# A two-layer hybrid decoder trunk on one core: the last steps of the attention gates at the scheduler's highest priority

## The chip, the cores and the metric

The kernel runs on one core of one Trainium2 chip. The metric is the device time of one execution in microseconds (us), as the median of several runs; lower is better. The core's engines are named as in the profile: PE (TensorE matmul), PEld (its weight loads), DVE (VectorE), ACT (ScalarE), POOL (GpSimd) and SP (SyncE, which here issues nearly all DMAs). A "q" behind an engine's name stands for its sequencer, so SPq is the queue from which SP issues its DMAs, one behind the other.

## The reference, cut to what matters

Two layers, sequence 1024, width 1024, all in float32:

```
h    = rms_norm(x, pre_gain) * (1 + scale) + shift
proj = h @ w_in            # split into q, k, v and gate of three head groups
a_out = sliding_window_attention(aq, ak, av, sinks) * silu(ag)
r_out = rms_norm(retention(rq, rk, rv)) * silu(rg)
g_out = rms_norm(gated_linear_attention(...)) * silu(gg)
y    = concatenate([a_out, r_out, g_out]) @ w_out
x    = x + gate * rms_norm(y, post_gain)
```

The change touches only `* silu(ag)`: the product of the attention's output with its gate, 512 of the 1024 columns of the concatenation.

## The kernel before, in words

**Numbers.** Every matmul operand is held as a high part (`fp32r`, a rounded copy) and a low part (the value minus its high part), and a product is three passes: high by high, low by high, high by low. So each activation that goes into a matmul passes through a cast and a subtraction, both on DVE for the gates.

**Tiles.** The sequence is 8 token tiles of 128. The mixed activations of a tile go through DRAM: `mixS` holds them split in high and low part, `mixF` holds them whole (only in the last layer, for tiles 2 to 7), `aoS` holds the attention's output before its gate, `xs` the residual between the layers.

**Order.** The PE instructions stand in the order in which the program writes them. A small planner inside the program decides that order: each unit of work is a generator ("job") that yields a delay or a flag to wait for, and `pump()` runs the jobs that are due on a clock that counts PE time only. The instructions of the other engines, the DMAs of SP's queue included, are placed by the tile scheduler: it takes of the instructions that it thinks ready the one with the highest priority, by default the one written earliest. Within an engine's queue the order is then fixed, and each instruction waits there for its semaphores while those behind it wait too.

**The gates.** `gate(g, hf, kk, pm)` handles 128 of the 512 gate columns (`k = 2*g + kk`) for four token tiles (half `hf`). It takes the projection from PSUM (`tanh` on ACT, L1583, and a DVE step, L1584), waits until the attention's output of the four tiles is in `aoS`, loads it into `ao` (a DMA of 256 KB, `lao`), and after a further delay does its last steps:

- the product `ao = th * 0.5 * ao` (L1590, DVE);
- in the last layer the store of the whole values to `mixF` (tiles 2 to 7 only);
- the cast to the high part `mh` (`copy("mg")`, L151, DVE) and the low part `ml` (L1602, DVE);
- two stores, of `mh` and of `ml`, to `mixS`;
- the flags `mix1`, on which the planner lets the output product of these tiles begin.

There are 16 gates, eight in each layer. All their stores go through SP's queue (`sm0`, `sm1`).

**The last layer's end.** `last_output` multiplies tiles 0 and 1 plainly and tiles 2 to 7 in three pairs (`Pair`), each by seven block products on sums and differences of the blocks. A pair's `parts()` loads four whole blocks from `mixF` (256 KB each); `sum()` builds four sums on DVE (L1305 to L1308); `early()` and `late()` split them into high and low part (cast on ACT, L149; low part on DVE, L1279); `a22()` loads a block of `mixS` in two halves (`a<-mixS`). `kept` (L1341) copies a product out of PSUM on ACT, `summed` adds banks on DVE (L1345), takes the squares on ACT (L1349) and multiplies by the gain (L1350). `finish` loads the residual (`t<-xs`), adds on DVE (L1248) and stores the output on ACT's queue (`out_dram<-t`).

The tiles of the prediction: `t_2055` and `t_2056` are the last two gates' `ao` (tiles 4 to 7); `t_2058`, `t_2059`, `t_2060` and `t_2061` are the four blocks of the first pair (tiles 2 and 3); `t_2066` and `t_2067` are the residual of tile 0; `t_2002` and `t_2003` are the two gates before the last two.

Of the kernel before, what the change touches and what calls it, by code (L numbers as in the profile page):

```python
# [93 lines left out]
def trunk(ctx: ExitStack, tc: tile.TileContext, ins, cst, out):  # L94
# [18 lines left out]
    def t2(dt=F32):  # L113
        return gp.tile([P, 512], dt, tag="t2", name=nm("t2"), bufs=B2)
# [16 lines left out]
    def f(ap):  # L131
        return ap.bitcast(F32)
# [11 lines left out]
    def eng(k):  # L144
        return G if EN[k] == "G" else V

    def copy(k, dst, src):
        if EN[k] == "A":
            A.activation(dst, src, AF.Copy)  # L149
        else:  # L150
            V.tensor_copy(dst, src)  # L151

    def dma(k, dst, src):
        {"S": nc.sync, "A": A, "P": G}[EN[k]].dma_start(dst, src)
# [28 lines left out]
    def lat(key, l):  # L183

        return L[key + "@1"] if l and key + "@1" in L else L[key]
# [4 lines left out]
    def flag(name, lat=0.0):  # L190
        flags[name] = clk[0] + lat
# [1274 lines left out]
    def layer(l):  # L1466
# [35 lines left out]
        for p in range(NP_):  # L1502
            last = p == NP_ - 1
            rr = {}
            for name in ("rq", "rk", "rv"):
                w = used(l, name)
                for tt in range(2):
                    t = 2 * p + tt
# [68 lines left out]
        def rows(d, hf, *i):  # L1577
            return d[(slice(4 * hf, 4 * hf + 4), slice(None)) + i].rearrange("t p q -> p t q")

        def gate(g, hf, kk, pm):  # L1580
            k = 2 * g + kk
            th = t2()
            A.activation(th, pm, AF.Tanh, scale=0.5)  # L1583
            V.scalar_tensor_tensor(th, th, 1.0, pm, ALU.add, ALU.mult)  # L1584
            for t in range(4 * hf, 4 * hf + 4):
                yield (0.0, ("ao", l, t, g))
            ao = t2()
            dma("lao", ao.rearrange("p (t q) -> p t q", t=4), rows(aoS, hf, k))
            yield lat("ag1", l)
            V.scalar_tensor_tensor(ao, th, 0.5, ao, ALU.mult, ALU.mult)  # L1590
            mh, ml = t2(F32R), t2(F32R)
            def tiles(x, ts):
                return x.rearrange("p (t q) -> p t q", t=4)[:, ts]

            ts = slice(0, 4)
            if l == DEPTH - 1:
                t0 = max(PLAIN - 4 * hf, 0)
                if t0 < 4:
                    dma("sm0", rows(mixF, hf, k)[:, t0:4], tiles(ao, slice(t0, 4)))
                ts = slice(0, min(t0 + 1, 4)) if t0 else slice(0, 4, 2)  # L1600
            copy("mg", tiles(mh, ts), tiles(ao, ts))
            eng("mgl").tensor_tensor(tiles(ml, ts), tiles(ao, ts), tiles(f(mh), ts), ALU.subtract)  # L1602
            for a, m in ((0, mh), (1, ml)):
                dma(f"sm{a}", rows(mixS, hf, a, k)[:, ts], tiles(f(m), ts))
            for t in range(4 * hf, 4 * hf + 4):
                flag(("mix1", l, t, k), lat("lay1", l))

        for hf in range(2):
            for g in range(2):
# [7 lines left out]
        for hf in range(2):  # L1617
            for g in range(2):
                for kk in range(2):
                    pm = mm()  # L1620
                    project_T(pm, l, hf, used(l, f"ag{g}"), kk * P)
                    job(gate(g, hf, kk, pm))
                    pump()
                if hf and not g:
                    if l == DEPTH - 1:
                        sw_first("W10")
                    else:
                        load(l, "o2")
            if not hf:
                if l == DEPTH - 1:  # L1630
                    sw_first("T1")
                    sw_first("W11")
                else:
                    load(l, "o0")
                    load(l, "o1")
# [86 lines left out]
```

## Time and profile before

| what | value |
|---|---|
| time, median of 3 runs | 998.21 us (996.72 to 999.19) |
| the profiled execution's own time | 996.31 us |
| its span, first to last instruction | 994.6 us |
| mean granted TensorE clock | 0.991 |
| PE busy | 965.7 us, 97% of the span |
| DVE, ACT, POOL busy | 683.2, 409.3, 246.3 us |

Times inside the kernel are us from the span's start. The groups by line show what an instruction costs, the windows show how busy each engine is in a stretch, the chain shows the work that ended last, followed back from the last instruction. On the chain an entry gives its start and how long it lasted.

### The profile page before, as it was taken

To read this page: it belongs to the slowest core of one execution; us is meant where nothing else is said; L and a number is where in the kernel's file an instruction comes from. 1 tells how busy PE (TensorE), PEld (TensorE's weight loads), DVE (VectorE), ACT (ScalarE), POOL (GpSimd) and SP (SyncE) were. 2 spreads that over 40 slices of the span, in tenths; PEclk is the share of its full clock that TensorE was granted. 3 is DMA by queue.
4 is the path that set the end of the run, shared out by engine and by line. 5 is a ranking of instruction groups with operands and counts; after the bars stand their busy time and mean duration, and the time that the engine had idled before them with its cause. 6 is when DMAs were issued, how large, how long until landed. Compare 5 with 4: busy or idle time off the path is not lost.

```text
span 994.6 us, 19641 instructions
## 1 busy us (share of the span) xinstructions
PE 965.7 (97%) x7133; PEld 824.3 (83%) x7133; DVE 683.2 (69%) x1679; ACT 409.3 (41%) x1152; POOL 246.3 (25%) x310
## 2 busy tenths in 40 slices
PE   5899999999999999999999999999999999999996
PEld 1599999888998777778889999988999877777785
DVE  3779857677766777664677286775766577567876
ACT  2477312233332656632555332133333257574222
POOL 2322001233310234420124101113322034545000
PEclk8899999999999999999999999999999999999999
DMA  9843513523135355587555241352122434378883
GB/s 321 290 138 97 159 44 115 177 86 121 61 100 166 91 157 168 170 274 239 189 170 171 69 150 38 118 157 83 53 93 86 127 91 133 112 235 266 267 262 139
DMA packets 112305, 148.77 MB, mean 150 GB/s; under 512 B 12065, under 2 KB 63821, under 8 KB 112209
## 3 DMA queue, kind: packets, MB, share of 16 engines
q1 hardware_dynamic: 106512, 137.96, 44.5%
q10 hardware_dynamic: 5696, 9.56, 2.6%
q8 instruction: 56, 0.92, 0.4%
q14 instruction: 41, 0.33, 0.1%
HBM read 109.20 MB, written 36.18 MB: 146 GB/s over the span
## 4 chain that ended last, share of the span: by engine, by line
PE 80%; DVE 7%; DMA 7%; issue 2%; POOL 1%; ACT 1%; SPq 0%; ACTq 0%; POOLq 0%; DVEq 0%
PE mm L165 61%; PE aux L165 14%; PE aux L180 5%; DMA st<-in_w_in_dram 2%; POOL sm L635 1%; DMA t<-aoS 1%; DMA st<-in_w_last_dram 1%; DMA xk<-in_x_dram 1%; DVE arena L533 1%; DMA a<-mixS 1%; DVE t L1248 0%; DVE t L328 0%; DMA t<-in_x_dram 0%; DMA t<-xs 0%; DMA mixS<-t 0%
## 5 line engine op out<-in xcount | busy, mean ns | idle before, releaser
L165 PE MATMUL mm<-arena 128*128 128x256 f32 (+2 forms) x1824 | 299.9, 318 | 1.8 <-ACT arena L704 1.8
L165 PE MATMUL mm<-arena,arena 128*128 128x256 f32 (+2 forms) x1824 | 298.2, 316 | 0.0
L165 PEld LDWEIGHTS mm<-arena 128*128 128x128 f32 x1824 | 255.5, 191 | 26.0 <-issue 3.3
L165 PEld LDWEIGHTS mm<-arena,arena 128*128 128x128 f32 x1824 | 252.2, 188 | 24.3 <-issue 3.7
L635 POOL TENSOR_TENSOR sm<-sm,mhalf 128x1 f32<-128x1 f32 (+1 forms) x64 | 55.8, 872 | 335.9 <-DVE sm L634 317.8
L165 PE MATMUL mm<-arena,mx 128*128 128x512 f32 (+1 forms) x564 | 130.6, 387 | 0.5 <-ACT kept L1341 0.5
L165 PEld LDWEIGHTS mm<-arena,mx 128*128 128x128 f32 x564 | 101.4, 188 | 24.7 <-issue 1.9
L149 ACT ACTIVATE t<-aux 128x256 f32<-128x256 f32 (+2 forms) x124 | 55.8, 468 | 73.8 <-PE aux L180 62.2
L149 ACT ACTIVATE arena<-st 128x512 fp32r<-128x512 f32 x94 | 56.2, 627 | 53.2 <-DMA st<-in_w_in_dram 19.4
L929 POOL TENSOR_TENSOR smx<-smx,sm 128x512 f32<-128x512 f32 x32 | 36.1, 1129 | 125.7 <-DVE sm L928 118.0
L533 POOL TENSOR_TENSOR arena<-st,arena 128x512 fp32r<-128x512 f32 x31 | 42.7, 1378 | 79.7 <-ACT arena L149 72.9
L533 DVE TENSOR_TENSOR arena<-st,arena 128x512 fp32r<-128x512 f32 x77 | 58.0, 775 | 5.2 <-ACT arena L149 3.3
L925 ACT ACTIVATE smx<-smx,sm 128x129 f32<-128x129 f32 x128 | 49.9, 393 | 25.9 <-DVE sm L922 25.7
L364 DVE SCALAR_TENSOR_TENSOR acc<-st,c_act,acc 128x512 f32<-128x512 f32 x60 | 46.7, 778 | 16.9 <-DMA st<-in_w_mod_dram 16.5
L180 PE MATMUL aux<-c_ident,t 128*128 128x128 f32 (+1 forms) x292 | 48.2, 282 | 5.4 <-DVE t L666 5.0
L180 PEld LDWEIGHTS aux<-c_ident,t 128*128 128x128 f32 (+1 forms) x292 | 35.0, 144 | 12.4 <-DVE t L666 6.9
L698 ACT ACTIVATE t<-aux,mod,mod 128x128 f32<-128x128 f32 x68 | 25.9, 459 | 43.0 <-DVE t L1248 18.1
L165 PEld LDWEIGHTS aux<-t,mx 32*128 32x128 f32 (+1 forms) x896 | 39.5, 187 | 3.9 <-issue 2.1
L973 ACT ACTIVATE t<-aux 128x256 f32<-128x256 f32 x32 | 12.3, 383 | 73.6 <-PE aux L165 65.0
L165 PE MATMUL aux<-t,mx 32*128 32x32 f32 (+1 forms) x896 | 40.7, 272 | 0.0
L920 DVE COPY_PREDICATED smx<-c_curmask,aux 128x256 f32<-128x256 int32 x64 | 25.4, 446 | 19.5 <-ACT smx L149 17.2
L1248 DVE SCALAR_TENSOR_TENSOR t<-t,sm,t 128x512 f32<-128x512 f32 x32 | 24.0, 780 | 18.2 <-DMA t<-in_x_dram 10.8
(224 smaller groups left out, 1387.7 us busy)
## 6 DMA issues: line engine op xcount, KB each, us to landing
st<-in_w_in_dram SPq DMA_DIRECT2D x96, 256.0 KB, 3.8
st<-in_w_mod_dram SPq DMA_DIRECT2D x64, 256.0 KB, 3.1
mx<-mixS SPq DMA_DIRECT2D x20, 512.0 KB, 4.9
mixS<-t SPq DMA_DIRECT2D x72, 128.0 KB, 3.7
st<-in_w_last_dram SPq DMA_DIRECT2D x36, 256.0 KB, 3.8
wm<-in_w_mod_dram SPq DMA_DIRECT2D x12, 512.0 KB, 7.0
t<-in_x_dram SPq DMA_DIRECT2D x24, 256.0 KB, 4.9
t<-tabS SPq DMA_DIRECT2D x16, 256.0 KB, 4.6
```

What stands on the lines that cost most here:

```text
L149: A.activation(dst, src, AF.Copy)
L165: T.matmul(dst, lhsT, rhs, start=start, stop=stop)
L180: T.transpose(dst, src, idn)
L364: V.scalar_tensor_tensor(acc, wt, c_act[:, k:k + 1], acc, ALU.mult, ALU.add)
L533: e.tensor_tensor(lo, st, f(hi), ALU.subtract)
L635: G.tensor_tensor(r, r, mhalf[:, :w], ALU.pow)
L698: A.activation(hf[:, ks], at[kt], AF.Identity, scale=gain, bias=shift)
L920: V.copy_predicated(sv, curmask.unsqueeze(1).to_broadcast((P, 2, P)), pv[:, :, n // P - 1, :])
L925: A.activation(sm[:, h, :], sm[:, h, :], AF.Exp, bias=mx[:, h:h + 1], accum_out=sums[:, h:h + 1])
L929: eng("pn").tensor_tensor(sm[:, :, 0:128], sm[:, :, 0:128], rs.unsqueeze(2).to_broadcast((P, 4, P)), ALU.mult)
L973: A.activation(sq, po, AF.Square)
L1248: V.scalar_tensor_tensor(xt[j], yg[j], r, xt[j], ALU.mult, ALU.add)
```

## The change

The last steps become a function `gate_out`, and it is called inside `tc.high_priority()`: whenever the scheduler thinks one of these instructions ready, it places it ahead of every other ready instruction of that engine. Nothing else is edited: the same instructions with the same operands, and the PE order is the same word for word. (The low part's line becomes L1608, the product's L1596.)

```
             ao = t2()
             dma("lao", ao.rearrange("p (t q) -> p t q", t=4), rows(aoS, hf, k))
             yield lat("ag1", l)
+            with tc.high_priority():
+                gate_out(hf, k, th, ao)
+            for t in range(4 * hf, 4 * hf + 4):
+                flag(("mix1", l, t, k), lat("lay1", l))
+
+        def gate_out(hf, k, th, ao):
             V.scalar_tensor_tensor(ao, th, 0.5, ao, ALU.mult, ALU.mult)
             mh, ml = t2(F32R), t2(F32R)
...
             eng("mgl").tensor_tensor(tiles(ml, ts), tiles(ao, ts), tiles(f(mh), ts), ALU.subtract)
             for a, m in ((0, mh), (1, ml)):
                 dma(f"sm{a}", rows(mixS, hf, a, k)[:, ts], tiles(f(m), ts))
-            for t in range(4 * hf, 4 * hf + 4):
-                flag(("mix1", l, t, k), lat("lay1", l))
```

What moves is little: no row on PE and POOL, and a few rows at each gate on DVE and SP. Three places matter below.

SP's queue in the last layer, at the last two gates (`t_2055`, `t_2056`) and the first pair's loads (`t_2058` and up; `-` stands before, `+` now):

```order
 L154 DMA t_2056_11464<-aoS 128x4x128
 L154 DMA t_2058_11470<-mixF 128x512
+L154 DMA mixF<-t_2055_11462 128x4x128
+L154 DMA mixF<-t_2056_11464 128x4x128
 L154 DMA t_2059_11472<-mixF 128x512
 L154 DMA t_2060_11474<-mixF 128x512
@@ -579,6 +581,4 @@
 L154 DMA t_2066_11493<-xs 128x512
 L154 DMA t_2067_11494<-xs 128x512
-L154 DMA mixF<-t_2055_11462 128x4x128
-L154 DMA mixF<-t_2056_11464 128x4x128
```

The two stores moved ahead of the last three of the pair's four loads and of the two residual loads; on DVE no row moved around this place.

SP's queue one step earlier, at the two gates before these (`t_2002`, `t_2003`; `t_2012` to `t_2015` are their high and low parts; `st` are the last layer's weights on their way in):

```order
 L154 DMA mixF<-t_2003_11197 128x4x128
+L154 DMA mixS<-t_2012_11255 128x2x128
+L154 DMA mixS<-t_2014_11263 128x2x128
+L154 DMA mixS<-t_2013_11256 128x2x128
+L154 DMA mixS<-t_2015_11264 128x2x128
 L154 DMA aoS<-t_2011_11239 128x256
-L154 DMA mixS<-t_2012_11255 128x2x128
-L154 DMA mixS<-t_2013_11256 128x2x128
-L154 DMA mixS<-t_2014_11263 128x2x128
-L154 DMA mixS<-t_2015_11264 128x2x128
 L154 DMA st_11370<-in_w_last_dram 128x512
```

The four stores moved ahead of one store of the attention's output, and the weight load stands behind all five as before.

ACT's queue at the first pair (`mx_11501` and `mx_11581` are the high parts of the sums, `kept_11613` the copy of the pair's first product):

```order
 L149 ACTIVATE mx_11501<-t_2060_11474 128x512
+L149 ACTIVATE mx_11581<-t_2058_11470 128x512
 L154 DMA out_dram<-t_2066_11493 128x512
 L149 ACTIVATE mx_11581<-t_2061_11476 128x512
 L154 DMA out_dram<-t_2067_11494 128x512
-L149 ACTIVATE mx_11581<-t_2058_11470 128x512
+L1341 ACTIVATE kept_11613<-mm_11600 128x512
 L1349 ACTIVATE st_11532,sm_11342<-t_2035_11344 128x512
-L1341 ACTIVATE kept_11613<-mm_11600 128x512
```

The copy of the first product moved ahead of a square, and one cast moved ahead of an output store.

More of the change, by code (lines that the diff above doesn't have):

```diff
@@ L1589, in gate, with gate_out @@
             yield lat("ag1", l)
+            with tc.high_priority():
+                gate_out(hf, k, th, ao)
+            for t in range(4 * hf, 4 * hf + 4):
+                flag(("mix1", l, t, k), lat("lay1", l))
+        def gate_out(hf, k, th, ao):
             V.scalar_tensor_tensor(ao, th, 0.5, ao, ALU.mult, ALU.mult)
@@ L1604, in gate @@
                 dma(f"sm{a}", rows(mixS, hf, a, k)[:, ts], tiles(f(m), ts))
-            for t in range(4 * hf, 4 * hf + 4):
-                flag(("mix1", l, t, k), lat("lay1", l))
         for hf in range(2):
```

## The prediction

> **What bounds the kernel now.** I read the page first: PE is the bound on average, so a change on DVE and SP can only count where PE waits.
>
> ```profile
> span 994.6 us, 19641 instructions
> PE 965.7 (97%) x7133; PEld 824.3 (83%) x7133; DVE 683.2 (69%) x1679; ACT 409.3 (41%) x1152; POOL 246.3 (25%) x310
> ```
>
> Next the windows, cut at the stretches in which the gates' steps lie: those of layer 0 from 370 to 440, those of layer 1 from 850 to 935. Each row gives the length, then the busy time of PE, PEld, DVE, ACT and POOL (with counts), the granted clock, the DMA share and GB/s.
>
> ```profile
> 330.00:405.00 75.00, 75.00 (x453) 56.25 (x452) 57.88 (x112) 47.50 (x147) 30.23 (x32) 1.00 0.50 154
> 405.00:440.00 35.00, 35.00 (x216) 25.65 (x215) 21.22 (x42) 16.75 (x58) 12.25 (x17) 1.00 0.68 198
> 440.00:520.00 80.00, 80.00 (x386) 65.18 (x385) 47.27 (x110) 33.80 (x92) 10.34 (x15) 1.00 0.63 211
> 850.00:885.00 35.00, 35.00 (x218) 24.91 (x215) 22.79 (x49) 22.94 (x79) 18.19 (x20) 1.00 0.55 169
> 885.00:905.00 20.00, 20.00 (x110) 14.60 (x109) 11.78 (x22) 10.25 (x27) 10.49 (x11) 1.00 0.82 248
> 905.00:945.00 40.00, 38.01 (x166) 29.51 (x165) 32.97 (x52) 14.45 (x29) 8.36 (x7) 1.00 0.81 257
> 945.00:994.60 49.60, 41.62 (x192) 33.86 (x190) 34.87 (x67) 12.37 (x32) 4.04 (x6) 0.96 0.63 200
> ```
>
> PE has no gap from 330 to 520 and from 850 to 905: whatever the gates' steps do there is under PE's cover, to gain or to lose, as long as nothing gets late by microseconds. PE first waits between 905 and 945, for 2.0 us, in the two places that PE's timeline shows in brackets:
>
> ```profile
> 931.79 3.04 PE L165 MATMUL mm<-arena,mx 128*128 128x512 f32 x12 [0.54 <-ACT kept L1341]
> 944.61 3.00 PE L165 MATMUL mm<-arena,a 128*128 128x512 f32 x12 [1.45 <-DMA a<-mixS]
> 983.74 2.88 PE L165 MATMUL mm<-arena,a 128*128 128x256 f32 x24
> ```
>
> From 944.61 to its last product (983.74 + 2.88 = 986.6) PE runs through, and the 8 us after that are the fixed end. So the time is set by when the load `a<-mixS` lands. The chain that ended last shows what that waited for; its entries are start, length, what:
>
> ```profile
> 901.77 2.98 DMA st<-in_w_last_dram
> ...
> 917.29 4.30 DMA t<-aoS
> ...
> 921.61 0.69 DVE t L1590
> ...
> 924.57 0.70 DVE t L1305
> ...
> 932.72 0.61 DVE t L1345
> ...
> 933.60 3.50 DMA t<-xs
> ...
> 937.16 7.31 DMA a<-mixS
> ...
> 944.61 11.50 PE mm L165 x48
> ```
>
> The last two gates' product (L1590) and the first pair's sum (L1305) stand on it one behind the other, and from 924.57 to 932.72 DVE is on the chain almost without a break. Whatever delays L1305 delays everything down to 944.61, and with it the end.
>
> **The change, part by part.** No instruction is added or removed; three moves count.
>
> *First, the stores ahead of the loads.* SP's timeline before, at this place:
>
> ```profile
> 917.29 0.92 SPq L154 DMA_DIRECT2D t<-aoS  x2
> 918.30 1.88 SPq L154 DMA_DIRECT2D t<-mixF  x4
> 922.33 1.52 SPq L154 DMA_DIRECT2D t<-xs  x2
> 923.90 0.98 SPq L154 DMA_DIRECT2D mixF<-t  x2
> 930.67 1.81 SPq L154 DMA_DIRECT2D mixS<-t  x3
> ```
>
> The four loads of the pair were issued back to back from 918.30 and waited for nothing. Now the two stores stand behind the first of them, and a store waits for its product on DVE:
>
> ```profile
> 920.12 1.14 DVE L1350 TENSOR_TENSOR t<-t,modg 128x512 f32<-128x512 f32 x1 [0.84 <-ACT st L1349]
> 921.61 0.69 DVE L1590 SCALAR_TENSOR_TENSOR t<-t,t 128x512 f32<-128x512 f32 x1 [0.34 <-DMA t<-aoS]
> 922.82 0.68 DVE L1590 SCALAR_TENSOR_TENSOR t<-t,t 128x512 f32<-128x512 f32 x1
> 924.57 0.69 DVE L1305 TENSOR_TENSOR t<-t,t 128x512 f32<-128x512 f32 x1
> ```
>
> The second product ends at 922.82 + 0.68 = 923.50. Its store then takes 0.49 to issue (0.98 for two), so the load of `t_2059` goes out at about 924.0 instead of 918.8. L1305 adds `t_2058` and `t_2059`, so it waits for that landing; `t_2060` and `t_2061` follow at 0.5 us each, and DVE needs them one and five steps later, so they add nothing. The residual loads follow behind and are needed last.
>
> How long does the load take? These rows of SP's timeline, the DMA lists and the tile's view bound it (in the lists the last number is the median from issue to landing, of the four loads issued in 918 to 921 and of those issued in 948 to 956; the tile's row covers every load and store of `mixF`):
>
> ```profile
> t<-mixF SPq DMA_DIRECT2D x4, 256.0 KB, 5.5
> t<-mixF SPq DMA_DIRECT2D x4, 256.0 KB, 3.3
> DMA to landing us min/median/max: 1.8/1.9/5.5
> 899.26 2.40 SPq L154 DMA_DIRECT2D mixS<-t  x4
> ```
>
> From below 1.8, the shortest landing of this tensor (issued at 924.0 it still comes after 924.57, so a gain is excluded here); from above 5.5, the same loads before, issued in one burst behind two others. The nearest row is the weight load at 901.77 on the chain: 256 KB, issued right behind four stores, 2.98. The loads at 948 to 956, spread out, took 3.3. I take 3.0: the two stores ahead are the same sort of traffic, and the burst's two loads from `aoS` have mostly drained by then. The product lands L1305 at 924.0 + 3.0 = 927.0, which is 2.4 later than 924.57; with the ends, 1.2 to 4.9 later.
>
> [...]
>
> *Second, the stores of the gates before.* The weight load at 901.77 waited for four `mixS` stores (899.26 + 2.40 = 901.66). These now go out as soon as their parts are made, ahead of an `aoS` store, and what the load then waits for is the sum that uses its slot:
>
> ```profile
> 899.17 0.43 DVE L1602 TENSOR_TENSOR t<-t,t 128x256 fp32r<-128x256 f32 x1
> 900.41 0.88 DVE L571 TENSOR_TENSOR st<-st,st 128x512 f32<-128x512 f32 x1 [0.82 <-DMA st<-in_w_last_dram]
> ```
>
> The last low part ends at 899.60, the sum at 901.29; the load goes out at about 901.3, a gain of 0.4 on the chain. It reaches L1590 at 921.61 only in part: DVE is in L1350 until 920.12 + 1.14 = 921.26, so the first product gains 0.3, and the second with it. The `aoS` store that is now last goes out some 1.5 us later; its reader is loaded at 917.29, long after.
>
> *Third, ACT's order.* PE's wait of 0.54 at 931.79 was for the copy `kept`, which stood behind a square (L1349) that waited for DVE. It is now ahead of that square, but behind an output store that waits for the same late DVE chain:
>
> ```profile
> 929.27 0.34 ACTq L154 DMA_DIRECT2D out_dram<-t  x1
> 931.16 0.58 ACT L1341 ACTIVATE kept<-mm 128x512 f32<-128x512 f32 x1
> ```
>
> With DVE later by 2.1, the store is issued until 929.27 + 0.34 + 2.1 = 931.7 and the copy starts 0.5 later than 931.16. PE's products up to 943.16 (944.61 less 1.45) then end at about 943.7, still ahead of the load `a<-mixS` at 944.48 + 2.1 = 946.6. So this move is covered by the load, and by nothing else if that landed early.
>
> *The other gates.* On DVE a product, cast or low part moves by one to four places, 0.3 to 1.5 us at the durations above, and SP's stores by one. They lie in the windows in which PE is never idle; I cost them at 0, covered by PE's own queue.
>
> **Sum.** +2.4 for the loads, less 0.3 for the earlier stores: +2.1. From L1305 on, DVE, the `mixS` stores at 930.67, the residual load at 933.60 and `a<-mixS` at 937.16 all keep their distances, since each waits for the one before. Against the execution's own 996.31 that is 998.4. This execution lies 1.9 below the median of the runs shown, so I add the difference to the median: 998.21 + 2.1 = 1000.3. With the ends of the landing: +0.9 to +4.6.
>
> **Rivals.**
>
> *Slower by more (R1).* The three loads behind two stores of 256 KB and ahead of two residual loads are again a burst, and land like the burst before, after 5.5. Then L1305 is 4.9 late, the sum +4.6, the time 1002.8. The point from which it counts as slower by over 0.3% (3.0 us, about what a measurement of this kernel can tell from no change) is a landing of 3.9. For it: DMA was the limit in this place, with the four loads at 5.5 each. Against it: 2.98 behind four stores at 901.77.
>
> *Hidden (R2), the change does not do in effect what its order says.* If `t_2059` had been the late part anyway (before, it could land no later than 924.57, after 5.8) and drops to 1.8, and the last load's 7.31 is set by the DMA engines' backlog and not by its issue, little is left: 998.2 to 999.1. Against it: the residual load before it is waited for by its own semaphore, 933.60 + 3.50 = 937.10, then 937.16.
>
> *Faster (R3).* The wait at 944.61 hangs on one landing of 7.31. If the later issue finds the DMA engines emptier, it could land like the loads of `ma<-mixS` that were issued beside it:
>
> ```profile
> ma<-mixS SPq DMA_DIRECT2D x4, 256.0 KB, 3.8
> ```
>
> Then PE starts at 943.7 instead of 944.61, as the third move has it: -0.9, or 997.3. It decides if the load lands in less than 5.2 (7.31 less 2.1). Against it: all traffic of that stretch moves together.
>
> *Room on PE upstream (R4).* The full windows could hide gaps between matmuls, which gate steps that come earlier would close. The rows that bear on it are the same products, 512 wide, in a long piece of the chain in layer 0 and in one at the very end:
>
> ```profile
> 468.16 11.18 PE mm L165 x48
> 958.91 16.64 PE mm L165 x72
> ```
>
> That is 0.233 and 0.231 each, so under 1% of the 245 us in the full windows, 2 us at most, is room; with the +2.1 it would give 998.2. [...] The two equal rates speak against it.
>
> **How the numbers follow.** Forecast 0.50, R1 0.30, R2 0.07, R4 0.05, R3 0.08. The three runs before spread over 2.5 us, so a median may lie 1.2 off. Slower by over 0.3%: nearly all of R1 and a quarter of the forecast (landings over 3.9, or the scatter), 0.40. Faster by over 0.3% asks for 3.0 us, more than R3 or R4 give without scatter: 0.06. Within: 0.54. The range runs from R3's 997.3 to R1's 1002.8 with its scatter, 1004.0.
>
> **What would show it.** In the changed profile: SP issues one `t<-mixF`, then two `mixF<-t` that wait for the product, then three `t<-mixF` from about 923.7; L1305 starts at 926 to 928 with a wait on `t<-mixF` in brackets; `a<-mixS` lands 2 us later and PE waits for it longer than 1.45; the windows from 330 to 520 stay full. The prediction is wrong if L1305 starts before 925.5 or after 928.5, if PE waits anywhere ahead of 905, or if PE at the end waits for something other than that load.

## The result, and the profile after

The changed kernel takes 1000.12 us (median of 21 runs, 997.02 to 1004.83), the kernel before 997.66 in the same comparison (21 runs, 995.54 to 1001.08). The ratio is 1.0025, with a 95% interval of 1.0013 to 1.0036, so the change costs about 2.5 us. The forecast was 2.1. The profiled execution of the changed kernel took 1001.09.

The page of the changed kernel begins almost as before, and the stretches that were full are still full. The windows give length, busy time of PE, PEld, DVE, ACT and POOL with counts, granted clock, DMA share and GB/s:

```profile
span 999.3 us, 19651 instructions
PE 966.8 (97%) x7133; PEld 825.0 (83%) x7133; DVE 682.8 (68%) x1679; ACT 409.6 (41%) x1152; POOL 247.2 (25%) x310
```

```profile
330.00:405.00 75.00, 75.00 (x451) 56.14 (x450) 57.70 (x110) 45.88 (x140) 29.88 (x31) 1.00 0.49 150
440.00:520.00 80.00, 80.00 (x382) 65.03 (x381) 46.59 (x109) 32.82 (x90) 9.89 (x15) 1.00 0.65 214
885.00:905.00 20.00, 20.00 (x110) 14.59 (x109) 14.35 (x23) 10.87 (x33) 9.88 (x11) 1.00 0.79 243
905.00:945.00 40.00, 37.27 (x157) 29.00 (x156) 28.20 (x45) 13.76 (x29) 9.69 (x9) 0.96 0.73 229
```

PE has no gap in the windows up to 905. Between 905 and 945 it now lacks 2.73 us where it lacked 2.0, and DVE is busy for 28.2 us of the 40 instead of 33.0. Of these 4.8 us DVE had done 2.6 already between 885 and 905 (14.35 against 11.78), so by 945 it is 2.2 behind. SP's timeline of the changed kernel (start, length, what) shows where that comes from:

```profile
921.06 0.45 SPq L154 DMA_DIRECT2D t<-mixF  x1
924.17 1.56 SPq L154 DMA_DIRECT2D mixF<-t  x2
925.79 1.48 SPq L154 DMA_DIRECT2D t<-mixF  x3
927.31 0.90 SPq L154 DMA_DIRECT2D t<-xs  x2
941.65 3.59 SPq L154 DMA_DIRECT2D a<-mixS  x2
```

SP stands still for 2.7 us behind its first `t<-mixF`, until the first of the two stores has its data. The three other loads go out at 925.79, one behind the other, and the residual loads behind them. DVE's timeline shows both sides of that wait, the two gates' products (L1596) and the first pair's sum (L1305):

```profile
923.46 0.69 DVE L1596 SCALAR_TENSOR_TENSOR t<-t,t 128x512 f32<-128x512 f32 x1 [0.19 <-DMA t<-aoS]
924.66 0.68 DVE L1596 SCALAR_TENSOR_TENSOR t<-t,t 128x512 f32<-128x512 f32 x1
929.00 0.69 DVE L1305 TENSOR_TENSOR t<-t,t 128x512 f32<-128x512 f32 x1 [2.51 <-DMA t<-mixF]
```

L1305 starts 929.00 − 923.46 = 5.54 us after the first product; before it was 924.57 − 921.61 = 2.96. This distance is the number to compare between executions, since it is free of the time at which an execution arrives here: 2.6 us are lost in this one step. PE's waits in its timeline, and the copy that releases the first of them:

```profile
934.41 0.60 ACT L1341 ACTIVATE kept<-mm 128x512 f32<-128x512 f32 x1 [0.42 <-DVE t L1248]
```

```profile
935.06 4.61 PE L165 MATMUL mm<-arena,mx 128*128 128x512 f32 x12 [2.73 <-ACT kept L1341]
949.58 3.00 PE L165 MATMUL mm<-arena,a 128*128 128x512 f32 x12 [1.55 <-DMA a<-mixS]
```

From these rows the 4.97 us by which PE's last run starts later (949.58 against 944.61) come out as follows. PE reached the first wait at 935.06 − 2.73 = 932.33, before at 931.79 − 0.54 = 931.25: 1.1 us that were there already. The wait for `kept` is 2.2 longer. The twelve products behind it take 4.61 instead of 3.04, 1.6 longer. The wait for the load `a<-mixS` is 0.1 longer. The 1.1 us belong to this execution, not to the change: the same PE row stands at 62.61 before and at 63.67 here, long ahead of the first gates at 370, and the run e7 below, which carries the whole change too, reached the same place at 932.57 − 2.12 = 930.45. The same 4.97 can be read along the chain through DVE and the load: the first product starts 1.85 later (923.46 against 921.61), L1305 loses 2.58, the way from there to the issue of `a<-mixS` is 0.06 longer, and the load, in the chain's row below, takes 7.80 instead of 7.31. On this path the slow twelve products do not appear, because PE had to wait for the load behind them. So the spans differ by 4.7 where the medians differ by 2.5.

```profile
941.65 7.80 DMA a<-mixS
```

### The profile page after: what moved, and what is told of

Its sections match the earlier page's. It is cut to its first block, busy times and chain, and to the rows that moved or that the text cites. A ratio compares the mean times of both kernels' runs of the same rounds, so it can differ in the third digit from the quotient of the medians.

```text
span 999.3 us, 19651 instructions
## 1 busy us (share of the span) xinstructions
PE 966.8 (97%) x7133; PEld 825.0 (83%) x7133; DVE 682.8 (68%) x1679; ACT 409.6 (41%) x1152; POOL 247.2 (25%) x310
## 4 chain that ended last, share of the span: by engine, by line
PE 82%; DVE 7%; DMA 6%; issue 2%; POOL 1%; ACT 1%; ACTq 0%; SPq 0%; POOLq 0%; DVEq 0%
PE mm L165 62%; PE aux L165 15%; PE aux L180 5%; DMA st<-in_w_in_dram 2%; POOL sm L635 1%; DMA xk<-in_x_dram 1%; DMA a<-mixS 1%; DMA t<-xs 1%; DVE arena L533 1%; DMA mixS<-t 1%; DVE t L328 0%; DVE t L1248 0%; DMA t<-in_x_dram 0%; DVE t L666 0%; DVE t L979 0%
## 5 line engine op out<-in xcount | busy, mean ns | idle before, releaser
L1248 DVE SCALAR_TENSOR_TENSOR t<-t,sm,t 128x512 f32<-128x512 f32 x32 | 24.1, 780 | 19.0 <-DMA t<-in_x_dram 12.2
```

Of the source, the lines that this page charges most:

```text
L1248: V.scalar_tensor_tensor(xt[j], yg[j], r, xt[j], ALU.mult, ALU.add)
```

## The experiments

Each run was compared with the kernel before on the same chip: median 997.70 for e1 to e4 (34 runs, 994.20 to 1002.28), 996.97 for e5 to e7 (29 runs, 993.59 to 1001.07), 996.68 for e8 and e9 (13 runs, 994.34 to 999.90). With this scatter, medians of 6 to 12 runs leave intervals of 0.1 to 0.2% to either side, 1 to 2 us.

| run | what it is | median us | ratio to before | 95% interval |
|---|---|---|---|---|
| e1 | high priority for the last two gates only | 1000.49 | 1.0026 | 1.0013 to 1.0038 |
| e2 | high priority for all gates but these | 997.36 | 0.9993 | 0.9983 to 1.0004 |
| e3 | before, the two `mixF` stores alone moved | 1000.47 | 1.0028 | 1.0014 to 1.0043 |
| e4 | after, these two stores alone left back | 997.80 | 1.0001 | 0.9985 to 1.0017 |
| e5 | after, the pairs' loads at high priority too | 998.99 | 1.0021 | 1.0009 to 1.0033 |
| e6 | before, `a<-mixS` from POOL's queue | 997.03 | 1.0001 | 0.9986 to 1.0015 |
| e7 | after, `a<-mixS` from POOL's queue | 998.85 | 1.0023 | 1.0012 to 1.0034 |
| e8 | before, `a<-mixS` ahead of the next pair's loads | 1000.92 | 1.0040 | 1.0027 to 1.0054 |
| e9 | e8 and e6 together | 1002.51 | 1.0060 | 1.0041 to 1.0078 |

**Which gates: e1 and e2.** The change is cut in two, by the condition under which `gate_out` gets the high priority. `hf and g` are the last two gates of a layer.

```
+            with tc.high_priority() if l == DEPTH - 1 and hf and g else ExitStack():        # e1
+            with tc.high_priority() if not (l == DEPTH - 1 and hf and g) else ExitStack():  # e2
                 gate_out(hf, k, th, ao)
```

> High priority for the last layer's last two gates alone (t_2055, t_2056); the other 14 gates as before. Theory (the two stores hold the loads back): the whole effect, ratio to before about 1.002 (+2 to +3 us); L1305 waits 2 to 3 us on t<-mixF, and the three held loads are issued about 5 us after the first. Rival (the loss comes from the other gates' moves, on DVE or at the stores around 900): ratio 1.000, and L1305 waits as well but the median does not move.

> High priority for the other 14 gates, the last two as before. Theory: ratio 1.000 (-0.3 to +0.6 us, the store order around 900), no wait of L1305, PE waits about 0.5 and 1.5 us as before. Rival (the other gates): ratio about 1.002 with the four loads of the pair issued back to back.

Two of sixteen gates carry the whole loss, and the other fourteen cost nothing that can be measured. SP's and DVE's timelines of e1, and then of e2:

```profile
925.12 1.48 SPq L154 DMA_DIRECT2D t<-mixF  x3
928.60 0.69 DVE L1305 TENSOR_TENSOR t<-t,t 128x512 f32<-128x512 f32 x1 [2.78 <-DMA t<-mixF]
```

```profile
917.37 1.95 SPq L154 DMA_DIRECT2D t<-mixF  x4
923.65 0.69 DVE L1305 TENSOR_TENSOR t<-t,t 128x512 f32<-128x512 f32 x1
```

In e1 the three loads stand apart from the first and L1305 waits 2.78 for one of them. In e2 all four go out together and L1305 waits for nothing: it starts 2.96 after the first product, exactly as before.

**Which of their steps: e3 and e4.** e3 is the kernel before with nothing but the two stores to `mixF` at high priority; e4 is the changed kernel with everything at high priority but these.

```
                 if t0 < 4:
+                    with tc.high_priority() if hf and g else ExitStack():          # e3
+                    with ExitStack() if hf and k > 1 else tc.high_priority():      # e4
                         dma("sm0", rows(mixF, hf, k)[:, t0:4], tiles(ao, slice(t0, 4)))
```

> Of the whole change only the two stores to mixF of the last two gates get the high priority; product, cast, low part and the stores to mixS are as before everywhere. Theory: these two DMAs are the whole effect, ratio about 1.002 (+2 to +3 us), L1305 waits 2 to 3 us. Rival (the DVE steps or the mixS stores matter): ratio 1.000.

> The changed kernel with the high priority taken from the two stores to mixF of the last two gates alone; everything else of the change stays. Theory: ratio to before 1.000 (-0.3 to +0.6 us), no wait of L1305 on t<-mixF, PE's waits as before. Rival (the rest of the change costs the time): ratio about 1.002.

Two DMA issues out of all that the change moves make the loss (e3), and without them no loss is left that can be measured (e4, between −1.5 and +1.7 us). e3, SP, DVE and PE:

```profile
922.20 1.56 SPq L154 DMA_DIRECT2D mixF<-t  x2
923.82 1.48 SPq L154 DMA_DIRECT2D t<-mixF  x3
927.22 0.69 DVE L1305 TENSOR_TENSOR t<-t,t 128x512 f32<-128x512 f32 x1 [2.71 <-DMA t<-mixF]
933.23 3.02 PE L165 MATMUL mm<-arena,mx 128*128 128x512 f32 x12 [2.09 <-ACT kept L1341]
946.43 3.34 PE L165 MATMUL mm<-arena,a 128*128 128x512 f32 x12 [0.82 <-DVE t L1307]
```

e4, SP and DVE:

```profile
918.74 1.87 SPq L154 DMA_DIRECT2D t<-mixF  x4
925.30 0.69 DVE L1305 TENSOR_TENSOR t<-t,t 128x512 f32<-128x512 f32 x1
```

**How much of it is L1305's own load: e5.** The four loads of each pair get high priority as well, and at the first pair the scheduler then leaves two of them, those that L1305 reads, ahead of the stores and two behind. (The line numbers of this kernel are one higher: its L1306 is L1305.)

```
+            with tc.high_priority():
+                self.p = mpart(o, 0), mpart(o, 1), mpart(e, 0), mpart(e, 1)
```

> The changed kernel with the pairs' four block loads at highest priority as well. In SP's queue the second block load (t_2059) of the first pair stands again ahead of the two stores; the third and fourth (t_2060, t_2061) still stand behind them. First theory (what costs is that L1305's own load stands behind a store that waits for DVE): L1305 starts with no wait on t<-mixF, and only L1306, which reads t_2060 and runs one step later, waits: issued about 924.5 to 925.5 with a landing of 3.0 it comes at about 927.5 to 928.5, where L1306 started about 1.7 us behind L1305 before, so DVE is late by about 1.5 to 2 at L1306 and the time is 0.15 to 0.2% above the kernel before. Rival (only L1305's place counts, since DVE has other steps to put in between): within 0.1% of the kernel before. Rival (any of the pair's loads behind a store costs the same): 0.25%.

```profile
924.81 0.95 SPq L154 DMA_DIRECT2D t<-mixF  x2
925.39 0.69 DVE L1306 TENSOR_TENSOR t<-t,t 128x512 f32<-128x512 f32 x1
928.42 0.69 DVE L1307 TENSOR_TENSOR t<-t,t 128x512 f32<-128x512 f32 x1 [0.90 <-DMA t<-mixF]
```

The first sum is on time, and the second takes its place as the late one: 928.42 is 5.99 after this execution's first product at 922.43, where the two stood 3.69 apart before (925.30 against 921.61), so 2.3 us are lost one step later. The time is 0.21% above, between the 0.15 to 0.2% of the first theory and the 0.25% of the second rival; the interval cannot tell these two apart. It shuts out "only L1305's place counts" (within 0.1%) but for its lower edge.

**What PE waits for at the end: e6 and e7.** One line: the loads `a<-mixS` issued from POOL's queue, in the kernel before (e6) and in the changed one (e7).

```
-                dma("lmix", f(hl[a]), mixS[self.o, :, a, 4:8])
+                G.dma_start(f(hl[a]), mixS[self.o, :, a, 4:8])
```

> The kernel before with the loads a<-mixS (L1315) issued from POOL's queue instead of SP's. It asks whether the end hangs on that landing. If it does: POOL is free at 935.8 where SP issued the load at 937.16, PE had waited 1.45 us for it, so the time falls by 0.5 to 1.4 us (0.05 to 0.14%), and PE's wait is then for DVE or gone. If the landing is set by the DMA engines' backlog: no change (within 0.05%). [...]

> The changed kernel with the loads a<-mixS (L1315) issued from POOL's queue. If the end hangs on that landing in the changed kernel too, PE's wait of 1.55 us for it goes or shrinks, and 0.5 to 1.5 us of the 2.5 us come back (ratio to the kernel before 1.0010 to 1.0020). If the delay of the loads sits on DVE's chain and would reach PE by another way (kept, or the next pair's sums), nothing comes back (ratio 1.0025).

POOL's and PE's timelines of e6, and the load in its chain:

```profile
934.69 1.30 POOL L1315 DMA_DIRECT2D a<-mixS  x2
944.25 2.10 PE L165 MATMUL mm<-arena,a 128*128 128x512 f32 x8 [0.70 <-DMA a<-mixS]
```

```profile
935.44 8.76 DMA a<-mixS
```

The load went out earlier (934.69 instead of 937.16, in an execution whose L1305 starts 1.0 earlier too) and took longer, 8.76 instead of 7.31, and PE still waited for it. The median did not move; a gain of up to 1.4 us lies within the interval, so whether the rest of a gain was there stays open. In e7 the load, issued at 937.99, is on time:

```profile
932.57 3.03 PE L165 MATMUL mm<-arena,mx 128*128 128x512 f32 x12 [2.12 <-ACT kept L1341]
942.38 3.02 PE L165 MATMUL mm<-arena,mx 128*128 128x512 f32 x12 [1.21 <-DVE t L1345]
948.59 5.86 PE L165 MATMUL mm<-arena,ma 128*128 128x512 f32 x24 [0.41 <-DVE t L1345]
```

PE no longer waits for that load at all, and what it waits for are DVE's sums (L1345): 1.21 and 0.41. No gain can be seen in the time, but the interval still allows one of about 1 us, so the median alone does not decide between the two cases of the expectation. The first of these waits is there with the load on SP's queue as well: PE waits 0.94 for L1345 in e1 and 0.74 in e3. By these traces the delay reaches PE by DVE's own chain as well as by the load, and the two are about equally long.

**An attempt at a faster kernel: e8 and e9.** As the load took longer in e6 though it was issued sooner (8.76 against 7.31), the next pair's four loads were written behind it, with the load on SP's queue (e8) and on POOL's (e9).

```
-            if nxt:
-                nxt.parts()
...
             a22 = cur.a22()
             if nxt:
+                nxt.parts()
                 nxt.sum()
```

> The kernel before, with the next pair's four block loads (parts) written behind the loads a<-mixS instead of ahead of them, so that in SP's queue a<-mixS stands ahead of three of these 256 KB loads. It asks whether the landing of a<-mixS (7.31 before, and 8.76 when POOL issued it earlier) is made of the loads issued just ahead of it. If so (three loads of 256 KB at some 390 GB/s are an estimate of 2.0 us), it lands 1.5 to 2 us sooner, PE's 1.45 us wait goes, and as DVE needs the next pair's blocks only about 5 us before PE does, the time falls by 1.0 to 1.45 us (ratio 0.9985 to 0.9990). Rival (the landing is set by all traffic that is in flight, not by the place in the queue): no change. Rival (the next pair's sums become late and PE waits for them): 1 to 2 us slower.

> As the run before, and the loads a<-mixS issued from POOL's queue as well, so that no other load of SP's stands ahead of them and they go out about 2 us sooner. If the loads ahead make the landing: PE's wait for it is gone altogether, ratio 0.9980 to 0.9990. If all traffic in flight makes it, or the next pair's sums become late: 1.000 or above.

e8, SP, DVE and PE:

```profile
937.23 0.90 SPq L154 DMA_DIRECT2D a<-mixS  x2
938.48 4.83 SPq L154 DMA_DIRECT2D t<-mixF  x3
946.49 0.69 DVE L1305 TENSOR_TENSOR t<-t,t 128x512 f32<-128x512 f32 x1 [4.63 <-DMA t<-mixF]
945.20 2.91 PE L165 MATMUL mm<-arena,a 128*128 128x512 f32 x12
950.36 5.86 PE L165 MATMUL mm<-arena,ma 128*128 128x512 f32 x24 [2.24 <-DVE t L1345]
```

The products with `a` start without a wait, but not because the load landed faster: it took 7.5 us from its issue, by the view of the tile `a`, where it had taken 7.31. It only went out earlier, 937.23 − 926.75 = 10.48 us after the first pair's L1305, where it had been 937.16 − 924.57 = 12.59. So three loads fewer ahead of it did not shorten the landing (the estimate of 2.0 us for them takes its rate from the kernel before, where the DMA engines moved 384 to 410 GB/s from 941.6 to 944.4). That fits the first rival, which no run tried by itself, and what the earlier place in the queue gained is the issue. And now the second pair's L1305 waits 4.63 for its block, and a sum behind it in DVE's queue (L1345), which PE needs, is late: PE waits 2.24 for it. It is the loss of this change once more, at the next pair. This trace does not hold all of e8's loss: its span is 4.8 us longer, but PE is 2.6 late already at 925 (925.33 against 922.71), most of it from a stretch near 670 at a granted clock of 0.50 for 6.8 us, on which the last section has more, so 2.2 are lost at the end where the medians differ by 4.2. e9 is worse: PE waits 0.58 for `a<-mixS` again, and 2.10 for DVE:

```profile
946.11 2.12 PE L165 MATMUL mm<-arena,a 128*128 128x512 f32 x8 [0.58 <-DMA a<-mixS]
950.33 5.86 PE L165 MATMUL mm<-arena,ma 128*128 128x512 f32 x24 [2.10 <-DVE t L1345]
```

The main expectation for both was wrong: "about 5 us" of slack counted the second pair's own products, not the sum of the first pair that is queued behind L1305. The rival that named late sums was right, and e8 lost more than its 1 to 2 us. No version here beats the kernel before; e2, e4 and e6 equal it within their intervals.

## Why the prediction was right, and where it was not

*First term, the stores ahead of the loads.* Right, and shown by e1 to e4 to be the whole effect, as far as intervals of 1 to 2 us can tell. Its size was 2.4; L1305 lost 2.6 in the changed kernel, 2.9 in e1 (928.60 against the first product at 922.79) and 2.8 in e3 (927.22 against 921.49). The mis-sized part is the landing, put at 3.0: it is 929.00 − 925.79 = 3.2 in the changed kernel, 3.5 in e1 and 3.4 in e3. The nearest row had been the right one to go by and the burst's 5.5 the wrong one, so the first rival (R1) falls. The lower end, 1.8, came from a row that counts stores and loads together; no load behind the moved stores came near it.

*"`t_2060` and `t_2061` ... add nothing."* True only beside a later `t_2059`: e5 shows that they cost 2.3 at the next sum by themselves.

*"The residual loads ... are needed last."* Off by a little. They are issued 5 us later, and DVE now waits for the first of them, which the working had at nothing:

```profile
931.97 0.75 DVE L1248 SCALAR_TENSOR_TENSOR t<-t,sm,t 128x512 f32<-128x512 f32 x1 [0.24 <-DMA t<-xs]
```

*Second term, −0.3 from the stores of the gates before.* Not seen. In e2, where these moved and the loads did not, the weight load goes out 900.40 − (897.90 + 0.43) = 2.07 after the last low part, before it was 901.77 − 899.60 = 2.17:

```profile
897.90 0.43 DVE L1608 TENSOR_TENSOR t<-t,t 128x256 fp32r<-128x256 f32 x1
899.45 0.89 DVE L571 TENSOR_TENSOR st<-st,st 128x512 f32<-128x512 f32 x1 [1.12 <-DMA st<-in_w_last_dram]
900.40 3.23 SPq L154 DMA_DIRECT2D st<-in_w_last_dram  x4
```

The step that failed took the room of one execution for that of the kernel. The load can gain only the time by which the stores ended after the sum L571, and L571 waits for its own weights: 0.82 in the execution that the 0.4 was read from, but 1.05 in e1 and 1.13 in e3, where these stores had not moved either, and there they ended only 0.20 and 0.16 after the sum. In e2 the wait is 1.12 and the gain 0.1. The medians cannot tell a term of this size. With 2.6 to 2.9 for the first term and 0.1 for this one the sum is 2.5 to 2.8, and the medians of after, e1 and e3 are 2.5, 2.8 and 2.8 above the kernel before (e7, with the load on POOL's queue, 1.9). The two errors do not cancel: a landing taken too short and a gain that did not come both made the forecast too small.

*Third move, ACT's order, "covered by the load".* It is no move of its own: ACT's rows stand in the new order in e1 and e3, in the old one in e2, so it follows from the two stores. The copy came later than I worked out: PE's wait for it grew from 0.54 to 2.73, and to 1.94 to 2.12 in e1, e3 and e7, where the working gives about 1.0. The copy stands behind an output store that waits for L1248, and everything that delays DVE adds up there: the landing's excess, the missing 0.3, the wait for the residual, and in the changed kernel's execution the 1.85 of its first product. In the changed kernel the load `a<-mixS` still covered it. But that PE at the end waits for that load says less than the prediction made of it. PE's last wait is for the load in the changed kernel (1.55) and in e1 (0.47 and 1.01). In e7 the load was early, PE waited for DVE's sums, and no gain could be measured. In e3 the trace names DVE's L1307 for the 0.82, a sum of the next pair that these products do not read, while their weight loads still wait 0.51 for the load, so e3 does not tell the two apart.

*The other gates at nothing.* Right, within the intervals of e2 and e4. The windows bore that out, but the reading that PE "first waits between 905 and 945" was too wide: outside the windows that it gives PE does wait, for instance 1.22 us at 669.66 before and 1.62 at 670.54 after, for a step of ACT.

*The rivals.* R1: no, the landing is 3.2 to 3.5. R2 (hidden): no, 2.5 us are lost. R3 (faster, by a quicker landing of `a<-mixS`): no; it took 7.80 instead of 7.31. R4 (room on PE upstream, 2 us at most): no sign of it, but not shut out; e2, which moves all the upstream steps and leaves out the loss, is at 0.9993, and its interval ends at 0.9983, a gain of 1.7 us.

*The checks by the clock.* L1305 started at 929.00, outside "926 to 928" and past the "928.5" that was to count against the prediction, and the three loads went out at 925.79 instead of 923.7. Counted from the first product it is 5.54 against a forecast of 2.96 + 2.4 = 5.4. The other checks held: one load, two stores, three loads on SP; no wait of PE in the windows ahead of 905; at the end the same load, with 1.55 instead of 1.45. The check of L1305 was badly put: absolute times carry an execution's own offset, here 1.1 us at PE and 1.85 at the first product, and distances between two instructions are free of it: from the first product to L1305 it is 2.96 before and in e2, 2.95 in e4 and 3.30 in e6, all with the stores behind the loads (in e6 L1305 waits 0.27 of it for a load).

## What to carry to other kernels

A high priority on a group of steps takes its DMAs along: a store that waits for a result, moved ahead of ready loads on SP's queue, made these loads wait for the result too (SP stood still for 2.7 us). It cost the time of the wait plus a landing (3.2 us), less what the loads had to spare: 2.6 us at L1305. Read the queue's order for what now stands behind each waiting entry, and count every load behind it, not only the one that is needed first. Before paying for a wait at the end of a chain, look for a second path of the same length: moving the load that PE waited for (e7) gave no gain that could be measured, and PE then waited for DVE's sums.

## What the runs showed of the hardware that was not expected

The twelve products after PE's wait of 2.73 us took 4.61 us instead of 3.04. The changed kernel's windows there, with the granted clock as the last number but two:

```profile
935.00:936.00 1.00, 0.94 (x3) 0.74 (x4) 1.00 (x4) 0.72 (x3) 0.00 (x0) 0.64 0.58 217
936.00:937.00 1.00, 1.00 (x4) 0.81 (x3) 1.00 (x3) 0.01 (x1) 0.00 (x0) 0.50 0.45 131
...
938.00:939.00 1.00, 1.00 (x4) 0.81 (x3) 0.75 (x3) 0.72 (x2) 0.00 (x0) 0.65 0.57 126
939.00:940.00 1.00, 1.00 (x6) 0.78 (x6) 0.83 (x3) 0.00 (x0) 0.05 (x1) 1.00 0.90 287
```

The granted clock is 0.50 for some 3.4 us (0.72 us of the first row, two rows in full with the one left out, 0.70 of 938 to 939) and then full again. After waits of 1.94 to 2.12 us at this place in e1, e3 and e7, and of 2.10 and 2.24 us some 16 us later in e9 and e8, the products took their usual time. They were slow again in e5, behind 2.50 us, and in e2, behind 1.93 and 0.20 us close together (eight products in 3.42 us, in e6 in 2.10). PE's timelines of e5 and of e2:

```profile
934.45 4.61 PE L165 MATMUL mm<-arena,mx 128*128 128x512 f32 x12 [2.50 <-ACT kept L1342]
```

```profile
944.19 1.17 PE L165 MATMUL mm<-arena,a 128*128 128x512 f32 x4 [1.93 <-DMA a<-mixS]
945.56 3.42 PE L165 MATMUL mm<-arena,a 128*128 128x512 f32 x8 [0.20 <-DMA a<-mixS]
```

The length of the wait does not decide alone. Near 670 us PE waits once for a step of ACT: behind 1.62 us in the changed kernel and 1.40 in e4 the twelve products that follow took 3.01 and 3.02 us, but behind 1.41 in e1 they took 4.28 and behind 1.96 in e8 5.47. The granted clock was 0.50 there for 3.4 us in e1 and for twice that, 6.8, in e8 (the means of these executions are 0.989 and 0.987, that of e4 0.991); in e2 and e5 above it was 3.4 again.

So the slow stretches came behind waits of 1.41 to 2.73 us in these rows, while none came behind others of up to 2.24 us, and what else decides was not tried. In the changed kernel the slow stretch lay under the landing of `a<-mixS`, which came 1.55 us after PE was ready; in e2 no wait followed it that could have covered it. How often it adds to the loss was not tried.

The same sum on DVE (L599, on the weights' way in) took 0.69 in e6 and 1.83 in e7, whose upstream part differs only by the order of the gates' steps. Beside it stands POOL's step L564 of the same execution:

```profile
909.48 0.69 DVE L599 TENSOR_TENSOR st<-st,st 128x512 f32<-128x512 f32 x1 [0.39 <-DMA st<-in_w_last_dram]
909.83 1.49 POOL L564 TENSOR_TENSOR arena<-st,arena 128x512 fp32r<-128x512 f32 x1 [1.29 <-ACT arena L149]
```

```profile
908.59 1.83 DVE L599 TENSOR_TENSOR st<-st,st 128x512 f32<-128x512 f32 x1 [0.76 <-DMA st<-in_w_last_dram]
908.58 1.29 POOL L564 TENSOR_TENSOR arena<-st,arena 128x512 fp32r<-128x512 f32 x1 [1.29 <-ACT arena L149]
```

In the eight traces in which POOL's step was already running when the sum started (before, e1 to e5, e7, e8) the sum took 1.07 to 1.83 us and ended 0.54 to 0.55 us after POOL's step, whenever it had started. With no POOL step running at its start (after, e6, e9) it took 0.69, and in e6, where POOL's step started 0.35 us behind the sum, that step took 1.49 instead of 1.29. No run moved the POOL step, so this is read from the times alone, and what makes the two steps longer was not shown. One sum differs by 1.1 us between executions in this way, which is why the conclusions above rest on medians and on distances.
